# A decoder layer on one core: earlier loads, transposes over two banks, and a projection done bank by bank

## The chip, the cores and the metric

The kernel runs on one core of a Trainium2 chip. The metric is the device time of one execution in microseconds, taken as the median of several runs. The engines have short names: PE (TensorE, matmuls and transposes; PEld is its weight load), ACT (ScalarE), DVE (VectorE), POOL (GpSimd), SP (SyncE, which issues the DMAs here).

## What is computed

One layer of a hybrid decoder over x of 2048 tokens by 1024 features, in float32. Both mixers share one input projection; their outputs share one output projection.

```python
u = rmsnorm(h, attn_pre_norm[i])
proj = u @ w_in[i]
hq, hf, hi, hg, sq, sk, sv = jnp.split(proj, splits, axis=-1)
o_hg = hgrn2_mix(hq, hf, hi, lb_all[i])                # gated linear recurrence, 4 heads of 128
o_hg = rmsnorm(o_hg, hg_out_norm[i]) * jax.nn.silu(hg)
o_sb = stick_breaking_mix(sq, sk, sv)                  # strictly causal attention, 8 heads of 64
o_sb = rmsnorm(o_sb, sb_out_norm[i])
mix = jnp.concatenate([o_hg, o_sb], axis=-1) @ w_out[i]
h = h + rmsnorm(mix, attn_post_norm[i])
u = rmsnorm(h, ffn_pre_norm[i])
gate, up = jnp.split(u @ w_gate_up[i], [D_FF], axis=-1)
y = (jax.nn.silu(gate) * up) @ w_down[i]
h = h + rmsnorm(y, ffn_post_norm[i])
h = h + (p[i] @ ple_proj[i]) * jax.nn.sigmoid(h @ ple_gate[i])
```

## The kernel before

The 2048 tokens are worked on in four groups (`GT` = 512 tokens, four tiles of 128). A matmul keeps float32 accuracy by splitting each operand into a high and a low part (`split`, `weight`: ACT casts the high part, DVE or POOL subtracts to get the low one, in turn) and adding three products (`mm3`, L221 to L223). So each weight tile of 128x512 costs one DMA, one cast and one subtraction; there are four raw buffers and three pairs for it.

The order on PE is the order of the code; the other engines' instructions are put in order by the framework's planner, which goes by an estimate of their times and by the buffers that are free. The code is written as generators ("streams"). `weave` runs one main stream and lets others step in between: a slot has two half slots, a main step follows each, and a stream with phase 0 or 1 steps only at every first or second half slot, while one with phase None is spread over all. `Rate` deals out the total number of steps of a stream over several weaves.

The stages that the change touches, in order of time, with names used below:

- start: `in_norm(0)` loads x of group 0, squares it with a sum (ACT), takes the root (POOL) and scales (ACT); `in_u` transposes it (L294, PE) into PSUM banks and splits it. Before all this `build_masks` makes small masks in a pool of its own that is closed again.
- a0, a1, a2, a3: input projection of a group for keys, queries, values. b0 to b3: the same for the recurrence's inputs. Beside them run the attention (`attention`: scores into "z", a scan on DVE, a product on POOL at L413, transposes into the bank "tr", evicted by ACT at L424 and DVE at L426, values into "av") and, from a2 on, the recurrence of a group (`hgrn`, 45 steps a group, all in the bank "hg"; a step's matmuls read products that POOL at L540 and DVE at L542 update after the step before).
- the joints: in the last three slots of b0 and b1, `in_u` for the group after the next, two chunks of four transposes per slot, all into "tr", the last two after the weave.
- o0 to o3: the output projection of a group (`out_proj`, operands loaded by `out_load`). It has 8 parts of 48 matmuls of 256 columns; a part takes two banks, loads two weight tiles one after the other, goes over both banks with each, and at its end evicts both (ACT at L643 or DVE at L645). After the first part the rows' sums of squares are formed in the bank "tr" (four one-column matmuls, two DVE copies, two POOL operations). Beside o0, o1 and the first half of o2 run the rest of attention and recurrence; beside o1, o2 and o3 the normalisation of the group before (`post_mix`), and in the second halves of o1 and o2 the turning of its result (`turn`, L688, also in "tr").
- then gate and up, down, and the gated embedding, which don't change.

There are eight PSUM banks: three "mm", two "z", one each of "av", "tr", "hg". SBUF tiles rotate by tag: "ev" has 12 buffers of 128x512 (evictions, mix, gb), "xt" has 8 (x, turned tiles, temporary results of gate_up).

Of the kernel before, what the change touches and what calls it, by code (L numbers as in the profile page):

```python
# [15 lines left out]
P = 128  # L16
# [44 lines left out]
def build_masks(nc, pool, masks):  # L61

    I32 = mybir.dt.int32

    def itile(name):
        return pool.tile([P, BL], I32, tag=name, name=name)
# [18 lines left out]
def hybrid_block(  # L85
# [77 lines left out]
    with tc.tile_pool(name="mtmp", bufs=1) as mtmp:  # L163
        build_masks(nc, mtmp, masks)
# [107 lines left out]
    def in_norm(g):  # L272
        toks = []
        for t in range(TT):
            halves = [xt(), xt()]
            r0 = g * GT + t * P
            for j in range(2):
                if g == 0:
                    with tc.high_priority():
                        nc.sync.dma_start(halves[j], x[r0:r0 + P, j * GT:(j + 1) * GT])  # L280
                else:
                    nc.sync.dma_start(halves[j], x[r0:r0 + P, j * GT:(j + 1) * GT])
            r = row_rstd(halves)
# [327 lines left out]
    def out_proj(g, res):  # L611
        ops, acc = res["o"], res["oss"]
        r_hg, r_sb = [], []
        mix = [[None, None] for _ in range(TT)]
        for quarter in range(4):
# [4 lines left out]
            for part in range(2):  # L620
# [7 lines left out]
                if quarter == 0 and part == 0:  # L628
                    b = bank("tr")
                    for t in range(TT):  # L630
                        nc.tensor.matmul(b[:, t:t + 1], acc[:, t * P:(t + 1) * P], ones1, start=True, stop=True)
                    rr = const.tile([P, 2 * TT], F32, tag="rg", name="rg", bufs=2)
                    nc.vector.tensor_copy(rr[:, 0:TT], hgss[:, g, :])
                    nc.vector.tensor_copy(rr[:, TT:], b[:, 0:TT])
                    nc.gpsimd.tensor_scalar(rr, rr, 1.0 / (HH * P), EPS, op0=ALU.mult, op1=ALU.add)
                    nc.gpsimd.tensor_tensor(rr, rr, neghalf.to_broadcast((P, 2 * TT)), op=ALU.pow)
                    r_hg = [rr[:, t:t + 1] for t in range(TT)]
                    r_sb = [rr[:, TT + t:TT + t + 1] for t in range(TT)]
                for t in range(TT):
                    b = banks[t // 2][:, t % 2 * 256:(t % 2 + 1) * 256]  # L640
                    d = mix[t][half][:, o * 256:(o + 1) * 256]
                    if part == 0:
                        nc.scalar.activation(d, b, AF.Copy, scale=r_hg[t])  # L643
                    else:
                        nc.vector.scalar_tensor_tensor(d, b, r_sb[t], d, op0=ALU.mult, op1=ALU.add)  # L645
                yield
        res["mix"] = mix

    def post_mix(g, mix):
        gb = [ev(name="gb") for _ in range(2)]  # L650
# [453 lines left out]
    class Rate:  # L1104
# [14 lines left out]
    u1 = Stream(in_u(in_norm(1), us[1], ["z", "av", "tr", "hg"]))  # L1119
    main = Stream(in_proj(0, us[0], KQV))  # L1120
# [9 lines left out]
    rest = units[3] - LAG  # L1130
# [3 lines left out]
        ("a", 3, 36, 21), ("b", 2, 48, 26), ("b", 3, 48, 38),  # L1134
# [3 lines left out]
    for n, (kind, g, att_n, hg_n) in enumerate(plan):  # L1138
# [4 lines left out]
        ra, rh = Rate(att_stream, 2, att_n, slots), Rate(hg, 1, hg_n, slots)  # L1143
# [5 lines left out]
        tail = 3 if nxt else 0  # L1149
# [7 lines left out]
        if n in (3, 5):  # L1157
            hg.drain()
    todo = total_units - spent + LAG + 1
    turned = []  # L1160
# [4 lines left out]
    tt0, tt1, ss0, ss1 = {}, {}, {}, {}  # L1165
    for g in range(NG - 1):
# [3 lines left out]
        if g == 0:  # L1170
            weave(op, 6, rates.part(6), r2.part(6, 1))
            hgs[2].drain()
            weave(op, OP_SLOTS - 6, rates.part(OP_SLOTS - 6), r3.part(OP_SLOTS - 6, 1))
        elif g == 1:
            weave(op, half, rates.part(half), r3.part(half, 1), (pm, TT, 0))
            tu = Stream(turn(un_s[0], u_s[0], g_ffn, "tr", xt, ev))
            weave(op, half, rates.part(half), r3.part(half, 1), (tu, 9, 0))
        else:
            weave(op, half, rates.part(half), r3.part(half, 1), (pm, TT, 0))
# [4 lines left out]
            mm_tags[:] = ["mm", "z", "mm", "z", "mm", "av"]  # L1184
            out_load(NG - 1, res[NG - 1])
# [87 lines left out]
```

## Time and profile before

| | us |
|---|---|
| median of 3 runs | 3137.79 |
| lowest, highest | 3131.59, 3140.38 |
| the profiled execution | 3140.98 |
| its span, first to last instruction | 3139.2 |

Everything in the next sections comes from the one profiled execution. Times in the trace count from the first instruction. A matmul's row covers its way through the array, so neighbouring matmuls overlap in the trace; what counts is when PE stands idle, and at which clock it runs (PEclk 1.00 is 2.4 GHz, 0.50 is 1.2 GHz; a stage's figure is a mean of the two).

### The profile page before, as it was taken

How to read it: one execution, taken by the hardware profiler on the slowest of the kernel's cores; microseconds unless marked ns; L12 is line 12 of the kernel's file. 1: busy time of each engine (PE TensorE's matmuls, PEld its weight loads, DVE VectorE, ACT ScalarE, POOL GpSimd, SP SyncE). 2: the span in 40 equal slices, each digit the busy share in tenths (PEclk: the TensorE clock that was granted, in tenths of full speed). 3: DMA queues.
4: the chain of work that ended last, by engine and by line, in shares of the span. 5: the costliest groups of instructions: out<-in, count | busy, mean ns of one | idle time of the engine just before them, and what ended most of it. 6: DMA issues, size and time to landing. Idle time of an engine off the chain costs nothing. (4 is left out here: it accounts for less than half of the span.)

```text
span 3139.2 us, 52948 instructions
## 1 busy us (share of the span) xinstructions
PE 2927.5 (93%) x18280; PEld 2455.3 (78%) x18280; DVE 2030.1 (65%) x2793; ACT 1587.0 (51%) x3187; POOL 1622.3 (52%) x1606
## 2 busy tenths in 40 slices
PE   7999899989999989778889999999999999998979
PEld 6888688868887878767767887888788888887757
DVE  3556566657677666654686677756786676746474
ACT  5666556656666666656543332355433333545432
POOL 3344355535556555755664444455744343657364
PEclk9999899989999999899999999999999999999989
DMA  6775465446445444546766676777855664678774
GB/s 189 224 212 163 128 182 162 146 134 174 150 142 156 145 138 118 182 134 228 239 219 208 228 246 220 225 230 221 290 185 186 204 217 132 220 221 278 253 258 148
DMA packets 463822, 607.02 MB, mean 193 GB/s; under 512 B 43456, under 2 KB 269760, under 8 KB 463552
## 3 DMA queue, kind: packets, MB, share of 16 engines
q1 hardware_dynamic: 463552, 603.63, 61.1%
q8 instruction: 144, 2.36, 0.3%
q14 instruction: 126, 1.03, 0.1%
HBM read 444.61 MB, written 158.86 MB: 192 GB/s over the span
## 5 line engine op out<-in xcount | busy, mean ns | idle before, releaser
L754 ACT CAST wh<-wr 128x512 fp32r<-128x512 f32 x600 | 354.1, 618 | 544.1 <-PE mm L222 165.6
L413 POOL TENSOR_TENSOR a<-be,ring 128x512 f32<-128x512 f32 (+2 forms) x320 | 314.0, 981 | 497.8 <-DVE ring L409 473.5
L755 POOL TENSOR_TENSOR wl<-wr,wh 128x512 fp32r<-128x512 f32 x256 | 370.4, 1454 | 360.9 <-ACT wh L754 343.6
L221 PE MATMUL mm<-uh,wh 128*128 128x512 f32 x1168 | 485.5, 416 | 4.4 <-DVE c L762 2.7
L223 PE MATMUL mm<-uh,wl 128*128 128x512 f32 x1168 | 461.8, 395 | 1.6 <-POOL wl L755 1.6
L222 PE MATMUL mm<-ul,wh 128*128 128x512 f32 x1168 | 461.2, 395 | 0.0
L755 DVE TENSOR_TENSOR wl<-wr,wh 128x512 fp32r<-128x512 f32 x344 | 313.0, 915 | 178.9 <-ACT wh L754 163.0
L221 PE MATMUL mm<-wh,uh 128*128 128x256 f32 (+1 forms) x1024 | 323.3, 316 | 9.0 <-ACT mix L643 6.4
L409 DVE TENSOR_TENSOR_SCAN ring<-z,ring,be 128x512 f32<-128x512 f32 x192 | 245.9, 1281 | 100.6 <-ACT z L395 96.9
L222 PE MATMUL mm<-wl,uh 128*128 128x256 f32 (+1 forms) x1024 | 306.7, 299 | 1.7 <-POOL wl L755 1.7
L223 PE MATMUL mm<-wh,ul 128*128 128x256 f32 (+1 forms) x1024 | 305.8, 299 | 0.0
L426 DVE TENSOR_TENSOR al<-tr,ah 128x512 fp32r<-128x512 f32 (+1 forms) x320 | 192.4, 601 | 113.3 <-ACT ah L424 112.6
L223 PEld LDWEIGHTS mm<-uh,wl 128*128 128x128 f32 x1168 | 222.2, 190 | 51.7 <-POOL wl L755 2.0
L221 PEld LDWEIGHTS mm<-uh,wh 128*128 128x128 f32 x1168 | 223.4, 191 | 46.9 <-DVE c L762 3.6
L207 ACT CAST wh<-wr 128x512 fp32r<-128x512 f32 x288 | 177.9, 618 | 151.9 <-PE mm L222 79.2
L222 PEld LDWEIGHTS mm<-ul,wh 128*128 128x128 f32 x1168 | 223.2, 191 | 38.6
L208 POOL TENSOR_TENSOR wl<-wr,wh 128x512 fp32r<-128x512 f32 x144 | 187.5, 1302 | 84.1 <-ACT wh L207 78.9
L394 ACT ACTIVATE be<-z 128x512 f32<-128x512 f32 (+2 forms) x320 | 170.9, 534 | 103.2 <-PE z L388 50.3
L221 PEld LDWEIGHTS mm<-wh,uh 128*128 128x128 f32 x1024 | 201.9, 197 | 17.8 <-ACT mix L643 7.2
L424 ACT CAST ah<-tr 128x512 fp32r<-128x512 f32 (+1 forms) x320 | 167.3, 523 | 95.6 <-PE tr L421 91.4
L222 PEld LDWEIGHTS mm<-wl,uh 128*128 128x128 f32 x1024 | 202.4, 198 | 7.3 <-POOL wl L755 2.0
L223 PEld LDWEIGHTS mm<-wh,ul 128*128 128x128 f32 x1024 | 201.9, 197 | 3.9
(287 smaller groups left out, 7256.5 us busy)
## 6 DMA issues: line engine op xcount, KB each, us to landing
wr<-in_w_gate_up_dram SPq DMA_DIRECT2D x308, 256.0 KB, 3.9
wr<-in_w_in_dram SPq DMA_DIRECT2D x224, 256.0 KB, 3.3
wr<-hid_s SPq DMA_DIRECT2D x154, 256.0 KB, 3.0
wr<-in_w_down_dram SPq DMA_DIRECT2D x110, 256.0 KB, 3.4
wr<-h_s SPq DMA_DIRECT2D x96, 256.0 KB, 4.3
hid_s<-hs SPq DMA_DIRECT2D x88, 256.0 KB, 3.1
wr<-wd_s SPq DMA_DIRECT2D x88, 256.0 KB, 3.5
kt<-k_s SPq DMA_DIRECT2D x80, 256.0 KB, 3.0
```

Source lines behind the costliest of these rows:

```text
L207: nc.scalar.copy(hi, src)
L208: (lo_engine or nc.gpsimd).tensor_tensor(lo, src, hi.bitcast(F32), op=ALU.subtract)
L221: nc.tensor.matmul(o, l[0], r[0], start=start, stop=False)
L222: nc.tensor.matmul(o, l[0], r[1], start=False, stop=False)
L223: nc.tensor.matmul(o, l[1], r[0], start=False, stop=stop)
L394: nc.scalar.activation(be[:, :n], z[:, :n], AF.Sigmoid, scale=0.125)
L409: nc.vector.tensor_tensor_scan(r[:, o:o + n][:, ::-1], z[:, :n][:, ::-1], be[:, :n][:, ::-1], init, op0=ALU.mult, op1=ALU.bypass)
L413: nc.gpsimd.tensor_tensor(a[:, :n], be[:, :n], r[:, o + 1:o + n + 1], op=ALU.mult)
L424: nc.scalar.copy(hi[:, lo_c:], tr[:, lo_c:])
L426: nc.vector.tensor_tensor(lo[:, lo_c:], tr[:, lo_c:], hi[:, lo_c:].bitcast(F32), op=ALU.subtract)
L754: nc.scalar.copy(hi, src)
L755: lo_engine.tensor_tensor(lo, src, hi.bitcast(F32), op=ALU.subtract)
```

## The change

- The masks are built after the x loads of groups 0 and 1, in a buffer of attention's tag "be"; their own pool is gone. For group 0 the scaling goes from ACT to DVE.
- At the joints the chunks go to "hg" and "tr" in turn; the recurrence has its steps before the joint.
- The plan gives attention 4 more units in a3, 4 in b2 and 6 in b3, and the recurrence 42 steps (38) in b3. The rest of both is spread over o0 and o1 alone (2.5 projections before). In b3, o0 and o1 the recurrence steps at half slots (phase None) instead of every second one.
- `dense_op` takes the place of `dense` in the output projection: both weight tiles are prepared first, then one bank is filled and evicted, then the other. The sums of squares come first.
- gb of `post_mix` lies in "xt" instead of "ev".
- o2 runs without attention and recurrence. The loads of group 3's operands stand at its start, and the first splits for gate_up step in its second half.

```diff
+    room = pool.tile([P, GT], I32, tag="be", name="room")
+    used = [0]
+
     def itile(name):
-        return pool.tile([P, BL], I32, tag=name, name=name)
+        used[0] += BL
+        return room[:, used[0] - BL:used[0]]
...
-    with tc.tile_pool(name="mtmp", bufs=1) as mtmp:
-        build_masks(nc, mtmp, masks)
...
+    def dense_op(w_cols, act):
+
+        ws = [weight(w_cols(kk)) for kk in range(0, HH, 2)]
+        banks = []
+        for i in range(2):
+            banks.append(mm_bank())
+            for kk in range(HH):
+                mv = [t[:, kk % 2 * 256:(kk % 2 + 1) * 256] for t in ws[kk // 2]]
+                for j in range(2):
+                    mm3(banks[i][:, j * 256:(j + 1) * 256], cut(act[kk], 2 * i + j), mv,
+                        kk == 0 and j == 0, kk == HH - 1 and j == 1)
+                if kk == 1:
+                    yield None
+            yield banks[i]
...
             for h in halves:
-                nc.scalar.activation(h, h, AF.Copy, scale=r)
+                if g == 0:
+                    nc.vector.tensor_scalar(h, h, r, None, op0=ALU.mult)
+                else:
+                    nc.scalar.activation(h, h, AF.Copy, scale=r)
...
+        sums(acc)
         mix = [[None, None] for _ in range(TT)]
...
-                for banks in dense(HH, src, ops[part * HH:(part + 1) * HH], False):
-                    if banks is None:
+                bank_no = 0
+                for b in dense_op(src, ops[part * HH:(part + 1) * HH]):
+                    if b is None:
                         yield
...
-        gb = [ev(name="gb") for _ in range(2)]
+        gb = [xt("gb") for _ in range(2)]
...
+    build_masks(nc, att, masks)
...
-        ("a", 3, 36, 21), ("b", 2, 48, 26), ("b", 3, 48, 38),
+        ("a", 3, 40, 21), ("b", 2, 52, 26), ("b", 3, 54, 42),
...
-        weave(main, slots - tail, ra.part(slots - tail), rh.part(slots - tail, 1))
+        weave(main, slots - tail, ra.part(slots - tail), rh.part(slots - tail, 1 if hg_n < slots else None))
+        if n in (3, 5):
+            hg.drain()
         if nxt:
-            un = Stream(in_u(toks, us[nxt], ["tr"]))
-            weave(main, tail, ra.part(tail), (un, 2 * tail, 0), rh.part(tail, 1))
+            un = Stream(in_u(toks, us[nxt], ["hg", "tr"]))
+            weave(main, tail, ra.part(tail), (un, 2 * tail, 0))
...
-    rates = Rate(att_stream, 2, todo, 2 * OP_SLOTS + OP_SLOTS // 2)
-    r2 = Rate(hgs[2], 1, HG_STEPS - 38, 6)
-    r3 = Rate(hgs[3], 1, HG_STEPS, 2 * OP_SLOTS + OP_SLOTS // 2 - 6)
+    rates = Rate(att_stream, 2, todo, 2 * OP_SLOTS)
+    r2 = Rate(hgs[2], 1, HG_STEPS - 42, 2)
+    r3 = Rate(hgs[3], 1, HG_STEPS, 2 * OP_SLOTS - 2)
...
-            weave(op, half, rates.part(half), r3.part(half, 1), (pm, TT, 0))
             hgs[3].drain()
             att_stream.drain()
             side.close()
             big[0] = ctx.enter_context(tc.tile_pool(name="bigr", bufs=1, side="right"))
             mm_tags[:] = ["mm", "z", "mm", "z", "mm", "av"]
+        else:
             out_load(NG - 1, res[NG - 1])
-            for prod in (1, 2):
-                for k in range(ND // 2):
-                    t_first(0, tt0, prod, k)
+            weave(op, half, (pm, TT, 0))
             tu = Stream(turn(un_s[1], u_s[1], g_ffn, "tr", xt, ev))
-            weave(op, half - 1, (tu, 9, 0))
+            weave(op, half, (tu, 9, 0), (Stream(first_operands()), ND, 1))
```

## Rows read from the trace of the kernel before

**Rows 1.** The page's first part: PE busy, share of the span.

```profile
PE 2927.5 (93%) x18280; PEld 2455.3 (78%) x18280; DVE 2030.1 (65%) x2793; ACT 1587.0 (51%) x3187; POOL 1622.3 (52%) x1606
```

**Rows 2.** Busy time by stage (start, a0, b0, b1, b3, o0-o3): from:to, length, engines, PEclk, DMA.

```profile
0.00:29.25 29.25, 7.38 (x33) 6.50 (x33) 12.48 (x28) 17.65 (x37) 10.45 (x39) 1.00 0.56 157
29.25:101.20 71.95, 70.85 (x422) 62.70 (x420) 22.63 (x35) 40.46 (x83) 21.51 (x30) 1.00 0.76 219
...
202.20:366.35 164.15, 149.04 (x831) 124.87 (x830) 92.53 (x124) 99.19 (x205) 67.10 (x73) 0.96 0.52 157
...
478.18:671.28 193.10, 180.50 (x1404) 149.43 (x1402) 123.83 (x174) 117.91 (x250) 95.69 (x125) 0.96 0.48 147
...
972.12:1168.07 195.95, 182.30 (x1754) 150.97 (x1752) 133.78 (x192) 124.21 (x259) 116.20 (x141) 0.98 0.47 139
1168.07:1268.57 100.50, 89.38 (x939) 80.89 (x938) 61.25 (x99) 62.14 (x137) 59.65 (x74) 0.96 0.44 131
1268.57:1398.09 129.52, 101.86 (x1041) 91.35 (x1039) 75.56 (x111) 80.41 (x179) 81.67 (x108) 0.91 0.48 155
1398.09:1492.97 94.88, 77.25 (x706) 72.31 (x704) 49.96 (x72) 58.73 (x126) 59.63 (x66) 0.89 0.64 217
1492.97:1556.48 63.51, 50.04 (x395) 49.14 (x394) 41.21 (x54) 34.48 (x79) 38.02 (x43) 0.92 0.75 251
```

**Rows 3.** Timeline of the start: start, length, engine, line, operation, idle before.

```profile
0.72 0.43 SPq L145 DMA_DIRECT2D g_pre<-in_attn_pre_norm_dram  x1
...
9.22 0.19 DVE L81 TENSOR_TENSOR mask<-ge,lt 128x32 uint8<-128x32 int32 x1
9.49 3.66 SPq L280 DMA_DIRECT2D xt<-in_x_dram  x8
9.84 0.69 DVE L208 TENSOR_TENSOR wl<-wr,wh 128x512 fp32r<-128x512 f32 x1 [0.42 <-ACT wh L207]
...
16.04 1.32 ACT L285 ACTIVATE xt<-xt,rstd 128x512 f32<-128x512 f32 x2
```

**Rows 4.** PE's waits in 202 to 671: who for whom, total us, times, longest.

```profile
PE tr L294 <- DVE ul L297: 14.9, 8, 2.8
PE tr L294 <- DVE al L426: 8.3, 5, 2.4
```

**Rows 5.** PE's waits in 972 to 1557 (b3 to o3).

```profile
PE hg L503 <- POOL qp L540: 13.6, 5, 5.7
PE tr L688 <- DVE al L426: 10.3, 6, 2.3
PE tr L688 <- ACT ev L694: 7.1, 3, 3.5
...
PE mm L221 <- ACT mix L643: 6.4, 2, 5.4
...
PE av L222 <- DVE wl L208: 3.6, 1, 3.6
...
PE z L222 <- DVE wl L208: 3.3, 1, 3.3
...
PE hg L503 <- DVE small L506: 1.9, 2, 1.0
```

**Rows 6.** Timeline of two recurrence steps in b3 and their last products.

```profile
1107.40 0.46 PE L503 MATMUL hg<-qp,ks 128*32 128x32 f32 x32
...
1108.41 0.81 POOL L540 TENSOR_TENSOR qp<-qp,tree 128x256 f32<-128x256 f32 x1
...
1127.93 1.05 PE L553 MATMUL hg<-v,q 128*128 128x128 f32 x8
...
1131.25 0.35 DVE L563 SCALAR_TENSOR_TENSOR sl<-st,tree,hg 128x128 f32<-128x128 f32 x1
```

**Rows 7.** Groups by line in o3 (1493 to 1557): count, busy us, mean ns, idle before.

```profile
L208 POOL TENSOR_TENSOR wl<-wr,wh 128x512 fp32r<-128x512 f32 x7 | 9.8, 1407 | 7.1 <-ACT wh L207 7.0
...
L208 DVE TENSOR_TENSOR wl<-wr,wh 128x512 fp32r<-128x512 f32 x7 | 8.0, 1147 | 0.5 <-ACT wh L207 0.5
```

More of the change, by code (lines that the diff above doesn't have):

```diff
@@ L613, in out_proj, with sums @@
         r_hg, r_sb = [], []
+        def sums(acc):
+            b = bank("tr")
+            for t in range(TT):
+                nc.tensor.matmul(b[:, t:t + 1], acc[:, t * P:(t + 1) * P], ones1, start=True, stop=True)
+            rr = const.tile([P, 2 * TT], F32, tag="rg", name="rg", bufs=2)
+            nc.vector.tensor_copy(rr[:, 0:TT], hgss[:, g, :])
+            nc.vector.tensor_copy(rr[:, TT:], b[:, 0:TT])
+            nc.gpsimd.tensor_scalar(rr, rr, 1.0 / (HH * P), EPS, op0=ALU.mult, op1=ALU.add)
+            nc.gpsimd.tensor_tensor(rr, rr, neghalf.to_broadcast((P, 2 * TT)), op=ALU.pow)
+            r_hg.extend(rr[:, t:t + 1] for t in range(TT))
+            r_sb.extend(rr[:, TT + t:TT + t + 1] for t in range(TT))
+        sums(acc)
         mix = [[None, None] for _ in range(TT)]
@@ L623, in src @@
                     return w_out[r:r + 2 * P, c:c + 256]
-                for banks in dense(HH, src, ops[part * HH:(part + 1) * HH], False):
-                    if banks is None:
+                bank_no = 0
+                for b in dense_op(src, ops[part * HH:(part + 1) * HH]):
+                    if b is None:
                         yield
[L628 to L646, printed above, removed]
+                        continue
+                    for n in range(2):
+                        t = 2 * bank_no + n
+                        d = mix[t][half][:, o * 256:(o + 1) * 256]
+                        bn = b[:, n * 256:(n + 1) * 256]
+                        if part == 0:
+                            nc.scalar.activation(d, bn, AF.Copy, scale=r_hg[t])
+                        else:
+                            nc.vector.scalar_tensor_tensor(d, bn, r_sb[t], d, op0=ALU.mult, op1=ALU.add)
+                    bank_no += 1
+                    yield
         res["mix"] = mix
     def post_mix(g, mix):
-        gb = [ev(name="gb") for _ in range(2)]
+        gb = [xt("gb") for _ in range(2)]
         for j in range(2):
@@ L1128, in hybrid_block @@
     hg_now = idle
-    rest = units[3] - LAG
     plan = [
@@ L1142, in hybrid_block @@
         hg = hgs[hg] if hg is not None else idle
-        ra, rh = Rate(att_stream, 2, att_n, slots), Rate(hg, 1, hg_n, slots)
+        tail = 3 if kind == "b" and g + 2 < NG else 0
+        ra, rh = Rate(att_stream, 2, att_n, slots), Rate(hg, 1, hg_n, slots - tail)
         spent += att_n
@@ L1148, in hybrid_block @@
             out_load(0, res[0])
-        tail = 3 if nxt else 0
-        weave(main, slots - tail, ra.part(slots - tail), rh.part(slots - tail, 1))
+        weave(main, slots - tail, ra.part(slots - tail), rh.part(slots - tail, 1 if hg_n < slots else None))
+        if n in (3, 5):
+            hg.drain()
         if nxt:
-            un = Stream(in_u(toks, us[nxt], ["tr"]))
-            weave(main, tail, ra.part(tail), (un, 2 * tail, 0), rh.part(tail, 1))
+            un = Stream(in_u(toks, us[nxt], ["hg", "tr"]))
+            weave(main, tail, ra.part(tail), (un, 2 * tail, 0))
             main.drain()
@@ L1156, in hybrid_block, with first_operands @@
         main.drain()
-        if n in (3, 5):
-            hg.drain()
     todo = total_units - spent + LAG + 1
-    turned = []
-    rates = Rate(att_stream, 2, todo, 2 * OP_SLOTS + OP_SLOTS // 2)
-    r2 = Rate(hgs[2], 1, HG_STEPS - 38, 6)
-    r3 = Rate(hgs[3], 1, HG_STEPS, 2 * OP_SLOTS + OP_SLOTS // 2 - 6)
+    rates = Rate(att_stream, 2, todo, 2 * OP_SLOTS)
+    r2 = Rate(hgs[2], 1, HG_STEPS - 42, 2)
+    r3 = Rate(hgs[3], 1, HG_STEPS, 2 * OP_SLOTS - 2)
     half = OP_SLOTS // 2
     tt0, tt1, ss0, ss1 = {}, {}, {}, {}
+    def first_operands():
+        for prod in (1, 2):
+            for k in range(ND // 2):
+                t_first(0, tt0, prod, k)
+                yield
     for g in range(NG - 1):
@@ L1170, in hybrid_block @@
         if g == 0:
-            weave(op, 6, rates.part(6), r2.part(6, 1))
+            weave(op, 2, rates.part(2), r2.part(2))
             hgs[2].drain()
-            weave(op, OP_SLOTS - 6, rates.part(OP_SLOTS - 6), r3.part(OP_SLOTS - 6, 1))
+            weave(op, OP_SLOTS - 2, rates.part(OP_SLOTS - 2), r3.part(OP_SLOTS - 2))
         elif g == 1:
-            weave(op, half, rates.part(half), r3.part(half, 1), (pm, TT, 0))
+            weave(op, half, rates.part(half), r3.part(half), (pm, TT, 0))
             tu = Stream(turn(un_s[0], u_s[0], g_ffn, "tr", xt, ev))
-            weave(op, half, rates.part(half), r3.part(half, 1), (tu, 9, 0))
-        else:
-            weave(op, half, rates.part(half), r3.part(half, 1), (pm, TT, 0))
+            weave(op, half, rates.part(half), r3.part(half), (tu, 9, 0))
             hgs[3].drain()
@@ L1184, in hybrid_block @@
             mm_tags[:] = ["mm", "z", "mm", "z", "mm", "av"]
+        else:
             out_load(NG - 1, res[NG - 1])
-            for prod in (1, 2):
-                for k in range(ND // 2):
-                    t_first(0, tt0, prod, k)
+            weave(op, half, (pm, TT, 0))
             tu = Stream(turn(un_s[1], u_s[1], g_ffn, "tr", xt, ev))
-            weave(op, half - 1, (tu, 9, 0))
+            weave(op, half, (tu, 9, 0), (Stream(first_operands()), ND, 1))
             for k in range(ND // 2):
```

## The prediction

> **What bounds the kernel now.** I read the page first: PE is busy 93% of the span, far ahead of the other engines [rows 1]. So time can be won only where PE stands idle or runs at the lower of its two clocks (1.2 instead of 2.4 GHz), and the next question is where. Busy time by stage answers it [rows 2]; idle is length minus PE busy. The start (to the first projection matmul) has 29.25 - 7.38 = 21.9 us. The two stages b0 and b1, whose ends transpose the next group's x (the joints), have 15.1 and 12.6, with a mean clock of 0.96. b3 has 13.7, and the four output projections o0 to o3 have 11.1, 27.7, 17.6 and 13.5, with clocks of 0.96, 0.91, 0.89, 0.92. These eight stages hold 133 us; the change touches each of them. What is lost to the clock I take as length x (1 - clock): b0 6.6, b1 7.7, b3 3.9, o0 to o3 4.0 + 11.7 + 10.4 + 5.1 = 31.2. It overlaps the idle time in part, so it is an upper bound. Then I asked, stretch by stretch, which wait ends last: at the start [rows 3], at the joints [rows 4], in b3 to o3 [rows 5, 6]; and what weights cost in o3 [rows 7]. The 1582 us after o3 (gate and up, down, gated embedding) keep their code.
>
> **Start.** SyncE issues the first x load at 9.49, right behind the last mask operation at 9.22, though its queue had begun at 0.72 [rows 3]: x lies where the mask builder's scratch lay. Without that pool the loads carry the highest priority and nothing holds them. Bounds: 8.8 earlier, if they go ahead of the six column loads at 0.72, and 0, if something else in the queue still holds them. I take 8 because of the priority mark, and since the columns that could go first are few. The eight scalings leave ScalarE (1.32 for two [rows 3], 5.3 in all), which also does eight squares; after the change the squares run at the pace of the landings, and only the last scaling stays on the path. I take 2 of the 5.3; bounds 0 and 5.3. A DVE scaling of this shape has no row; nearest is a DVE subtraction of 128x512 at 0.69 [rows 3], about ScalarE's 0.66. The mask work moves behind group 1's x loads: two POOL iotas and 20 DVE operations, about 8 us on DVE, in a stage where PE is busy 70.85 of 71.95 [rows 2] and DVE 22.63; cost nothing. If the cover failed, those 8 us would delay DVE evictions there. First users: attention, which gets its scratch buffer back, 70 us later. The weight loads now stand behind 2 MB of x; they are needed only after the transposes. **-10 us** (-2 to -14).
>
> **Joints.** Two chunks of transposes (L294) follow each other in a slot into the single "tr" bank, which attention also uses: the first waits for attention's eviction (L426: 8.3 us in 5 waits), the second for the first's (L297: 14.9 in 8) [rows 4]. Such pairs come four times per joint; these waits are 23 of the 27.7 us that b0 and b1 idle. With "hg" and "tr" in turn the first chunk goes at once and the second finds "tr" free about when the first does today: the second wait goes, the first stays. The recurrence must leave "hg" first: its last 24 steps run in 29 slots instead of 32, still at most one per slot, and cost nothing. I take 16 of 23 us (bounds 8 and 20), and 7 of the 14.3 us of clock (bounds 2 and 12). **-23**.
>
> **Recurrence at half slots.** A step's matmuls need the products that the step before released on POOL and DVE. Today steps fall on one half slot in two; where a rate exceeds one per slot, two stand back to back. Counting the rates: 6 such pairs in b3 (38 steps in 32 slots), 1 + 11 in the projections (7 in 6, 45 in 34). The trace has exactly 18 waits in the seven rows of "hg", 38.4 us together, of which the first and the last stand in [rows 5]. Afterwards no two share a half slot, but 52 of the 90 steps follow in the next one (20 in b3, 32 in o0 and o1), some 2.8 us of PE work later (b3: 182.3 / 64; o0: 89.4 / 32 [rows 2]). An ordinary step is ready 1.8 us after its start (1107.40 to 1109.22), so it fits; the state chain takes 3.7 (1127.93 to 1131.60) and does not [rows 6]. Estimate: 5 of the 52 are state chains, late by 0.9, and a fifth of the others is late by 1.5, since POOL and DVE are busy 60% here: 19 us. **-19** (bounds -34 and +16).
>
> **Output projection by banks.** Today a part fills two of three banks and evicts both at its end, so the next part soon meets a bank not yet released: 6.4 us in two waits, 5.4 of it in o3 [rows 5]. The 5.4 also holds a shortage of "ev" buffers, which moving gb to "xt" eases. Both go: **-6**. The price is in the weights. Of three pairs of buffers two now serve the whole part: a part's second weight reuses a pair freed 24 matmuls before its need, where today it is 48. At 50.04 us for 384 in o3 [rows 2] that is 3.1 us for a ScalarE cast and a subtraction; every second weight goes to POOL, 1.41 there [rows 7]. On ScalarE the cast waits in order, and the squares and evictions behind it wait too. In o0 and o1 attention and recurrence double the 3.1. In o2 and o3, 16 parts, I take 0.5 us each: **+8** (0 to +40). Means of 1.15 on DVE and 1.41 on POOL in o3 [rows 7], against 0.69 for a DVE subtraction at the start [rows 3], say that the two subtractions hinder each other. The Trainium skill (SBUF — State Buffer, "Who interferes with whom") has the rule that speaks against this change: a VectorE instruction with two SBUF inputs and a GpSimd instruction reading SBUF exclude each other, and the later one waits out the whole of the other. The means in [rows 7] agree. By the rule a POOL subtraction that waits out one of DVE ends 0.69 + 1.41 = 2.1 us after the cast, still under 3.1, and the sum stays; with more in front of it, it is rival A.
>
> **The row sums first.** Four one-column matmuls, two DVE copies and two POOL operations move to each projection's head. Their input was loaded one projection earlier. Attention's wait for their bank stays, at another place: 0.
>
> **Attention over two projections.** Fourteen units (4 in a3, 4 in b2, 6 in b3) and a few recurrence steps leave the projections for stages where PE is the bound: the same PE work elsewhere, 0. o2 loses attention and recurrence. Left on PE there: 46 us of matmuls (at most the 50.04 of o3) and 3 of transposes. ScalarE had 58.7 busy there and POOL 59.6 [rows 2]; without attention and recurrence but with all of the loads of group 3 (moved to o2's start, eight loads ahead of post_mix's in SyncE's queue) I estimate 47 to 50 each. Three engines of equal load don't mesh fully: **+8** (0 to +15). The 7.1 us in which o2's turning transposes waited for ScalarE [rows 5] came from two turns in one slot; now there are eight slots for nine: **-7** (-7 to 0). In o1 the 10.3 us behind attention's eviction [rows 5] stay.
>
> **gb in "xt"** (8 buffers): gb and four tokens want ten, so later tokens' loads wait for earlier ones. No matmul of o1 to o3 waits for them; where post_mix of group 3 meets gate_up, which uses "xt" too, 0, bounds -8 and +8.
>
> **Clock in b3 to o3:** 35 us today with 84 us idle. The idle falls by about a third: **-10** (-20 to 0).
>
> **Sum:** -10 - 23 - 19 - 6 + 8 + 8 - 7 - 10 = -59. The profiled execution took 3140.98 (span 3139.2), so 3082; it lay 3.2 above the median, so 3079 for the median.
>
> **Rivals.** A: slower. The 3.1 us don't suffice and nearly every part stalls on its second weight as o3 did twice, 3.6 and 3.3 us [rows 5], though it had double the slack. o3 lost 5.1 us of clock on 13.5 idle, 0.38 per us. 24 parts (o2, o3 and half of o0 and o1) x 3.5 x 1.38 = 116, instead of +8: 3079 + 108 = 3187. It turns slower from about 2.0 us of wait per part (24 x 2.0 x 1.38 = 66 eats 59 + 8). For it: the means in [rows 7]. Against: in o0 and o1 other matmuls stand in between, and o3 had two such waits in eight parts, not eight. B: the half slot is too short. Half of the 52 close steps wait 2.1 us like a pair today: 55 instead of 19, 3115. For it: DVE and POOL 60% busy; against: the 1.8 us. C: the moves do less than they say; x still goes behind columns and weights (-5), and the joints stay bound by attention's eviction (-8 in all): 3079 + 5 + 15 = 3099. D: gains and new waits cancel, about 3138.
>
> **How the numbers follow.** Forecast 0.74, A 0.06, B 0.09, C 0.06, D 0.05. A measurement of this kernel tells some 0.3% (9.4 us) from nothing. Faster: forecast, B and C, 0.89; same: D, 0.05; slower: A, 0.06. The term bounds give 3030 to 3140 if all fall on one side; the forecast's own spread is about 3045 to 3110, and with B and C inside 3045 to 3115 leaves out A, D and the tails.
>
> **What would show it.** Right: first x load before 5 us, first projection matmul near 19; at the joints one wait per pair, on attention's eviction; few waits above 2 us on "hg"; no wait on mix; o2 near 62 us, o0 to o3 together near 345 instead of 388. Wrong: many waits of o2 and o3 on wl or wh (A); dozens of short waits on "hg" (B); x loads after weights (C).

## The result, and the profile after

The changed kernel takes 3111.1 us (median of four runs, 3108.9 to 3112.1), the kernel before beside it 3134.7 (3129.9 to 3140.4): a ratio of 0.9923, interval 0.9903 to 0.9943. So it is faster, by 24 us, and the range held the time; but the forecast was 3079, a gain of 59. The profiled execution took 3112.1 (span 3110.3), where 3082 was forecast for it. The 30 us between the two are what has to be found.

The first part of the page, which answers to [rows 1]: busy time, share of the span, instructions. PE's share rose by one point.

```profile
PE 2918.1 (94%) x18280; PEld 2440.2 (78%) x18280; DVE 2034.7 (65%) x2801; ACT 1584.4 (51%) x3180; POOL 1632.3 (52%) x1606
```

Busy time by stage, as [rows 2], for the start, a0 to b3, o0 to o3, and all that follows: from:to, length, then busy time and instructions of PE, PEld, DVE, ACT and POOL, PEclk, DMA share, GB/s.

```profile
0.00:20.82 20.82, 7.50 (x32) 6.62 (x33) 8.91 (x34) 12.93 (x28) 10.93 (x39) 1.00 0.65 169
...
194.88:349.80 154.92, 146.25 (x832) 123.17 (x829) 89.31 (x122) 97.33 (x202) 67.14 (x73) 0.98 0.55 165
349.80:459.12 109.32, 108.35 (x1033) 92.03 (x1032) 72.24 (x111) 68.98 (x147) 56.55 (x72) 1.00 0.62 178
459.12:640.97 181.85, 175.50 (x1403) 146.00 (x1401) 125.10 (x174) 117.57 (x250) 95.39 (x125) 0.99 0.52 156
640.97:777.92 136.95, 134.60 (x1176) 111.20 (x1175) 98.94 (x144) 90.25 (x196) 73.34 (x96) 1.00 0.56 157
777.92:962.61 184.69, 178.41 (x1431) 146.84 (x1430) 130.15 (x174) 124.03 (x260) 107.97 (x128) 1.00 0.49 146
962.61:1163.44 200.83, 194.46 (x1849) 157.17 (x1840) 145.13 (x208) 135.74 (x286) 126.68 (x150) 0.99 0.49 143
1163.44:1265.49 102.05, 92.70 (x1048) 83.46 (x1047) 70.90 (x110) 64.18 (x140) 71.37 (x87) 0.97 0.42 129
1265.49:1379.13 113.64, 93.49 (x1038) 83.87 (x1038) 61.52 (x100) 68.43 (x150) 72.44 (x89) 0.94 0.49 163
1379.13:1461.78 82.65, 55.40 (x426) 53.97 (x426) 26.83 (x38) 46.26 (x97) 45.85 (x53) 0.83 0.69 231
1461.78:1522.96 61.18, 51.77 (x387) 49.75 (x386) 42.92 (x54) 33.56 (x77) 40.25 (x45) 0.94 0.80 265
1522.96:3110.34 1587.38, 1510.31 (x6634) 1238.77 (x6632) 1079.56 (x1406) 619.02 (x1120) 801.62 (x575) 0.97 0.68 219
```

The start is 8.4 us shorter, b0 9.2, b1 11.2 and a2 between them 2.5. a3 to b3 are 25.7 us longer: that is the attention moved there, with four recurrence steps (PE is busy 26.0 us longer in the three). o0 to o3 take 359.5 us instead of 388.4; 345 were forecast, and one row misses by more than those 14.5 us: o2 takes 82.65 us instead of the 62 of the forecast, PE stands still in 27 of them, and its clock is 0.83. The other parts of the 30 us: a3 and b2 idle 8.6 instead of 1.7, the stages behind o3, whose code is the same, are 4.7 longer, and the start is 1.6 short of its mark.

The waits of PE in b0 to b1 (as [rows 4]) and in b3 to o3 (as [rows 5]): who waits for whom, total us, times, longest.

```profile
PE tr L314 <- DVE al L446: 6.6, 5, 2.0
PE tr L441 <- DVE ul L317: 6.3, 5, 2.0
...
PE tr L715 <- DMA xt<-un_s: 15.6, 2, 12.6
PE av L458 <- DVE al L446: 8.2, 7, 3.2
PE z L224 <- POOL wl L210: 7.9, 6, 3.4
PE av L224 <- POOL wl L210: 7.5, 1, 7.5
...
PE hg L523 <- POOL qp L560: 6.3, 3, 4.0
PE tr L715 <- DVE al L446: 3.2, 2, 1.6
```

The second chunk's wait at the joints (14.9 us in [rows 4]) is gone and the first chunk's stayed, at 6.6; attention now waits 6.3 for "tr" in its turn (0.9 before). All waits on "hg" come to 13.6 us in 11 (18 waits and 38.4 us in [rows 5]), and no wait on mix is left. What is new is the first of these rows in b3 to o3: the transposes of `turn` wait 15.6 us for a DMA from `un_s`, the normalised rows that `post_mix` writes to DRAM.

**What o2 waits for.** PE's three long waits in o2, and rows of the other engines ahead of them: start, length, operation, idle before and its releaser.

```profile
1396.64 5.38 POOL L782 TENSOR_TENSOR ul<-wr,uh 128x512 fp32r<-128x512 f32 x4
1398.81 0.19 ACT L275 ACTIVATION_READ_ACCUMULATOR junk<-h 128x1 f32 x1
...
1401.98 1.71 POOL L210 TENSOR_TENSOR wl<-wr,wh 128x512 fp32r<-128x512 f32 x1
1403.75 0.58 PE L224 MATMUL av<-wl,uh 128*128 128x256 f32 x1 [7.54 <-POOL wl L210]
...
1408.64 0.33 POOL L277 TENSOR_TENSOR ssum<-ss 128x1 f32<-128x1 f32 x2
...
1413.10 1.34 ACT L692 ACTIVATE mix<-h,rstd 128x512 f32<-128x512 f32 x2 [2.26 <-POOL rstd L269]
1419.56 0.41 PE L715 MATMUL tr<-ident,xt 128*128 128x128 f32 x2 [2.94 <-DMA xt<-un_s]
1420.19 1.33 ACT L692 ACTIVATE mix<-h,rstd 128x512 f32<-128x512 f32 x2 [0.51 <-POOL rstd L269]
1426.99 1.33 ACT L692 ACTIVATE mix<-h,rstd 128x512 f32<-128x512 f32 x2 [0.47 <-POOL rstd L269]
1427.74 0.93 SPq L693 DMA_DIRECT2D un_s<-mix  x2
1429.85 3.44 SPq L703 DMA_DIRECT2D xt<-un_s  x7
1432.59 0.69 PE L715 MATMUL tr<-ident,xt 128*128 128x128 f32 x2 [12.62 <-DMA xt<-un_s]
```

Read from below. The transposes at 1432.59 need the load of 1429.85, that needs the store of 1427.74, and that the scaling of the group's last token tile at 1426.99. The last three of the four tiles come through this chain about 7 us apart (1413.10, 1420.19, 1426.99): square, row sum and root on ACT and POOL, gain on DVE, addition on POOL, square and root again, scaling on ACT. The first was scaled at 1388.71, and the second came late: ACT had its sums at 1399.00, and POOL adds them only at 1408.64, behind a run that is mostly subtractions for the first operands of gate and up (L782; two other operations of 128x512 stand among them). The same run delays a weight's low part and so the matmul at 1403.75. Before the change PE had attention and recurrence to do over this chain, and no matmul of o2 waited for `un_s`; now the chain lies bare.

### The profile page after: what moved, and what is told of

Read it like the earlier page. It is cut to its first block, busy times and chain, and to the rows that moved or that the text cites. A ratio compares the mean times of both kernels' runs of the same rounds, so it can differ in the third digit from the quotient of the medians.

```text
span 3110.3 us, 52961 instructions
## 1 busy us (share of the span) xinstructions
PE 2918.1 (94%) x18280; PEld 2440.2 (78%) x18280; DVE 2034.7 (65%) x2801; ACT 1584.4 (51%) x3180; POOL 1632.3 (52%) x1606
## 5 line engine op out<-in xcount | busy, mean ns | idle before, releaser
L782 POOL TENSOR_TENSOR wl<-wr,wh 128x512 fp32r<-128x512 f32 x256 | 370.5, 1454 | 369.6 <-ACT wh L781 360.4
L782 DVE TENSOR_TENSOR wl<-wr,wh 128x512 fp32r<-128x512 f32 x344 | 314.1, 919 | 167.3 <-ACT wh L781 145.6
L223 PE MATMUL mm<-wh,uh 128*128 128x256 f32 (+1 forms) x992 | 309.7, 312 | 2.3 <-ACT wh L781 2.2
L224 PE MATMUL mm<-wl,uh 128*128 128x256 f32 (+1 forms) x992 | 294.0, 296 | 2.9 <-POOL wl L782 2.6
L225 PE MATMUL mm<-wh,ul 128*128 128x256 f32 (+1 forms) x992 | 292.9, 295 | 0.0
L223 PEld LDWEIGHTS mm<-uh,wh 128*128 128x128 f32 x1168 | 221.7, 190 | 44.6 <-issue 2.6
L223 PEld LDWEIGHTS mm<-wh,uh 128*128 128x128 f32 x992 | 191.7, 193 | 10.7 <-ACT wh L781 3.1
L224 PEld LDWEIGHTS mm<-wl,uh 128*128 128x128 f32 x992 | 192.2, 194 | 8.7 <-POOL wl L782 3.6
L225 PEld LDWEIGHTS mm<-wh,ul 128*128 128x128 f32 x992 | 191.7, 193 | 3.8
```

What stands on the lines that cost most here:

```text
L223: nc.tensor.matmul(o, l[0], r[0], start=start, stop=False)
L224: nc.tensor.matmul(o, l[0], r[1], start=False, stop=False)
L225: nc.tensor.matmul(o, l[1], r[0], start=False, stop=stop)
L782: lo_engine.tensor_tensor(lo, src, hi.bitcast(F32), op=ALU.subtract)
```

## The experiments

All times are medians, their ratios are to the kernel before, and each kernel is the changed one with the edit shown.

**The first operands' subtractions off POOL** (e_first_vec):

```diff
-            tt[prod, k] = pair_of(t_blk(grp, prod - 1, 0, k), "u", prod, G)
+            tt[prod, k] = pair_of(t_blk(grp, prod - 1, 0, k), "u", prod, V)
```

> The changed kernel, with the subtractions of gate_up's first operands (products 1 and 2, eight of 128x512) in o2 on DVE instead of POOL. Theory POOL order: those eight stand ahead of a weight's subtraction and of post_mix's roots on POOL; they make both the 7.5 us wait and the 12.6 us wait of o2 (82.7 us long). Both together fall below 4, o2 comes to 62 to 66, the whole to 3111 - 18 = 3093. Theory dependency: the turn of group 1 is asked for before post_mix's chain through DRAM (some 7 us for each of four tokens) can be done, whatever POOL does. The 7.5 goes, 8 or more of the 12.6 stay, o2 about 73, the whole 3101.

**The turn after the first operands** (e_turn_late):

```diff
-            weave(op, half, (tu, 9, 0), (Stream(first_operands()), ND, 1))
+            weave(op, half // 2, (Stream(first_operands()), ND, 1))
+            weave(op, half // 2, (tu, 9, None))
```

> The changed kernel, with the turn of group 1 in the last four slots of o2 instead of the last eight; POOL keeps its work. Theory dependency: the waits of the turning transposes (2.9 and 12.6) fall below 4 together, the 7.5 on the weight stays, o2 about 69, the whole 3111 - 13 = 3098. Theory POOL order alone: post_mix is so late that half of the 12.6 is only met later, o2 76, the whole 3105.

Measured: 3105.4 (ratio 0.989 to 0.992) and 3104.5 (0.9887 to 0.9919), some 6 us better than the changed kernel each, with intervals that overlap its own. In e_first_vec, the stage o2, and what the turn waits for in it:

```profile
1378.91:1454.59 75.68, 53.32 (x426) 51.96 (x426) 33.88 (x46) 45.85 (x97) 38.00 (x45) 0.86 0.77 253
```

```profile
PE tr L715 <- DMA xt<-un_s: 19.3, 2, 17.0
```

```profile
1426.12 0.69 PE L715 MATMUL tr<-ident,xt 128*128 128x128 f32 x2 [16.97 <-DMA xt<-un_s]
```

In e_turn_late, the stages o2 and o3, and the same wait:

```profile
1376.65:1447.74 71.09, 56.14 (x426) 54.08 (x426) 26.48 (x37) 46.38 (x96) 48.57 (x55) 0.90 0.75 256
1447.74:1512.25 64.51, 51.32 (x387) 48.93 (x386) 41.15 (x56) 33.79 (x78) 38.12 (x43) 0.95 0.78 266
```

```profile
PE tr L715 <- DMA xt<-un_s: 1.4, 1, 1.4
```

With POOL free, the 7.5 us wait for the weight's low part is gone (1.0 is left) and o2 is 7 us shorter, but the turn waits 3.7 us more than before: PE came earlier to the same chain. The chain itself ends sooner: its second tile is scaled at 1399.60 instead of 1413.10, its last at 1420.10 instead of 1426.99, and the turn goes on at 1426.12 instead of 1432.59; those 6.5 us are o2's gain. So neither theory holds alone, and 3105.4 is above what either gave: POOL's order made the chain some 7 us longer, and the rest of its length stays. With the turn later, the wait for the chain falls from 15.6 to 1.4 and o2 by 11.6 us, of which o3 gives back 3.3; the wait for the weight's low part stays (7.6), as the first theory said. That is the chain shown as the cause of the turn's wait. The kernel gains only 6.6 of it; the profiled execution, the longest of its four runs (3109.0), is 7.6 us longer behind o3, and I can't say why, the code there is the same.

**Attention again over two and a half projections** (u_att), **and the plan's numbers alone** (p_plan: the first edit without the rest):

```diff
-        ("a", 3, 40, 21), ("b", 2, 52, 26), ("b", 3, 54, 42),
+        ("a", 3, 36, 21), ("b", 2, 48, 26), ("b", 3, 48, 42),
...
-    rates = Rate(att_stream, 2, todo, 2 * OP_SLOTS)
+    rates = Rate(att_stream, 2, todo, 2 * OP_SLOTS + OP_SLOTS // 2)
...
+        else:
+            weave(op, half, rates.part(half), (pm, TT, 0))
             att_stream.drain()
...
-        else:
             out_load(NG - 1, res[NG - 1])
-            weave(op, half, (pm, TT, 0))
```

> The changed kernel with attention's plan of before (36, 48, 48 units) and its rest over two and a half projections; the recurrence stays as changed. Theory: the two-projection plan only moves PE work (26 us into a3, b2, b3) and pays for it with new waits there (7 us) and in o2 (20 us), so undoing it shortens a3, b2, b3 by 25 to 33, lengthens o0 to o2 by about as much less some 10 to 15 us of waits: the whole 3097 to 3103. Rival (the prediction's own sum, in which this part cost nothing net): 3111 within 4.

> The attention part split: only its plan numbers go back (36, 48 and 48 pieces in a3, b2 and b3 instead of 40, 52 and 54), the attention still ends with the second output projection. With the whole part undone the stages lost 18.8 us, all of it waits: 10.3 in a3 to b3, 14.4 in o2, and o0 and o1 gained 4.6 of waits. Theory 'two costs': a3 to b3 lose their 10 us of waits, o0 and o1 (fourteen more pieces) take back 3 to 6, o2 keeps its 27 us of waits and its length of 80 to 84: 3104 to 3108. Rival 'the plan alone': o2 shortens too, 3093. Rival 'the waits only move': o0 and o1 take back all 10 us, 3109 to 3113.

Measured: 3092.7 (0.9846 to 0.9879) and 3104.4 (0.9885 to 0.9923). This part of the change costs 18 us, more than either theory had: without it the kernel is faster, by intervals that don't touch. The stages a3, b2 and o2 of u_att:

```profile
642.71:769.94 127.23, 127.18 (x1141) 106.74 (x1140) 92.70 (x135) 84.63 (x184) 69.40 (x91) 1.00 0.56 161
769.94:943.18 173.24, 171.59 (x1409) 142.90 (x1407) 121.81 (x165) 115.78 (x243) 99.98 (x121) 1.00 0.50 155
...
1360.55:1443.43 82.88, 70.05 (x484) 66.65 (x484) 34.38 (x48) 50.26 (x104) 45.24 (x50) 0.86 0.64 215
```

Set the last row against o2 of the changed kernel: 82.88 us with 70.05 of PE work, and 82.65 with 55.40. The 14.65 us of attention that were taken out of o2 bought nothing there; PE waits in their place, and they are paid a second time where they went. In a3 and b2 that is more than their own work, too: PE idles 8.6 us there in the changed kernel and 1.7 here. The row for it, in a3 and b2 of the changed kernel:

```profile
PE av L458 <- DVE al L446: 7.4, 16, 0.9
```

Sixteen short waits for DVE's low parts of attention's weights: with 13 pieces in eight slots or a little more, instead of 12, DVE comes late with some of them. What it does ahead of them I did not look up. In p_plan a3 and b2 idle 1.8 us, as in u_att, but its o2 has the fault of the changed kernel:

```profile
1370.43:1450.84 80.41, 57.28 (x426) 56.11 (x426) 25.36 (x40) 45.51 (x97) 45.08 (x52) 0.85 0.72 237
```

So "the plan alone" is out. Against "the waits only move": PE idles 6.8 us less in a3 to b3 than in the changed kernel and only 1.5 more in o0 and o1. By medians 6.7 of the 18.4 us are the plan's and 11.7 those of an o2 without attention, each some 3 us uncertain. The 11.7 is clear of noise (the intervals of p_plan and u_att don't touch), the 6.7 is not by itself: the intervals of p_plan and the changed kernel overlap. The 11.7 shows in o0 and o1, which carry o2's attention in p_plan and are 11.1 us longer there than in u_att, while its o2 is only 2.5 shorter.

**The gain rows again in "ev"** (u_gb), where mix and the evictions lie, **and the same without the attention part** (c_att_gb):

```diff
-        gb = [xt("gb") for _ in range(2)]
+        gb = [ev(name="gb") for _ in range(2)]
```

> The changed kernel with gb of post_mix in ev again. Theory: gb in xt holds two of eight buffers that gate_up's first temporaries need too, so the last tokens of group 3's post_mix load late; the waits at the start of gate_up (4.6 and 16.8 us) fall to the 13 us in all that stood there in the kernel before, and o3 gets its 5 us wait on mix back: the whole 3111 - 8 + 5 = 3108. Rival: those waits come from the order of t_second's work on ACT and DVE; then they stay near 21 us and the whole is 3116.

> The attention part undone and the gain rows of post_mix again in their own buffers (ev). Theory 'xt is short at the start of gate_up': the 16.9 us wait of the first gate_up product falls to some 6, the rest is near 1580 instead of 1588, and the kernel takes 3085 to 3089. Rival 'the gain rows cost nothing': 3091 to 3095, the gate_up wait is 16 to 17 again.

Measured: 3104.4 (0.9891 to 0.9924) and 3081.0 (0.9815 to 0.9844). Against u_att the second gains 11.7 us, and the intervals don't touch. PE's waits in the 77 us behind o3, of the changed kernel and of c_att_gb:

```profile
PE av L223 <- ACT wh L781: 21.4, 2, 16.8
```

```profile
PE av L225 <- DVE wl L782: 6.5, 2, 5.7
PE av L223 <- ACT wh L781: 6.4, 1, 6.4
```

The wait of 16.8 us for one weight of gate and up is 6.4 without the two "xt" buffers for gb (all waits there: 14.8 instead of 21.4), and the stages behind o3 take 1581.0 us instead of 1588.4 in u_att; where the other 4 of the 11.7 us come from these rows don't tell. `post_mix` of group 3 and gate and up draw on the same eight buffers, and the loads stand in one queue. Which of the loads is held up I did not single out, so that buffers are short there is the likely reason, not one that is shown. The theory of the second run holds for the wait and for the stages behind o3; both times came out lower than expected. In "ev" gb has a price too, which the change had taken away: in o2 and o3 of u_gb PE waits for mix again.

```profile
PE mm L223 <- ACT mix L669: 11.1, 2, 8.2
```

With attention in o2 (c_att_gb) this wait is 2.0. In the changed kernel the two prices of gb stand against each other: "ev" is 6.7 us better by medians, with intervals that overlap.

**The two edits of o2 once more, in c_att_gb** (c_att_gb_vec, c_att_gb_late):

> As the one before, and the subtractions of gate_up's first operands go from POOL to DVE. In the kernel without the attention change o2 has 14 us of waits of the output projection for POOL's low parts of the weights. Theory 'order on POOL': these fall to 4 or less and o2 is 8 to 10 us shorter, 3077 to 3081. Rival 'DVE, which still has the attention's low parts in the first half of o2, is late instead': less than 3 us, 3083 to 3089.

> As the second, and in the second half of o2 the first operands come first and the turn after them. In the kernel as changed this brought o2 from 82.7 to 71.1 us, since the turn stood waiting for the chain of post_mix through DRAM. Without the attention change no matmul of the turn waits for that chain any more (no such row in o2). Theory 'the attention covers the chain': nothing is left to gain, 3084 to 3091, and the last turn is pushed into o3. Rival 'the order helps for itself': 3077 to 3081.

Measured: 3080.8 (0.9801 to 0.9847) and 3079.4 (0.9804 to 0.9837), which the intervals don't tell from the 3081.0 of c_att_gb. With attention over the chain its wait in c_att_gb is 4.7 us and no more:

```profile
PE tr L715 <- DMA xt<-un_s: 4.7, 1, 4.7
```

So neither POOL's order nor the place of the turn is worth anything that the medians show. Both times lie in the ranges of the theories that gave the order a price of its own (3077 to 3081), but only because c_att_gb, without either edit, lies there as well. The theory of an order on POOL had counted on 14 us of waits for low parts; in o2 of c_att_gb there are 3.7, and 0.3 with the edit. In the profiled executions o2 is some 6 us shorter with either edit (77.2 and 76.1 for 82.8); as the four runs of the first spread from 3072.8 to 3085.8, a gain of that size is neither shown nor ruled out.

**The parts undone one at a time.** u_joint:

```diff
-            un = Stream(in_u(toks, us[nxt], ["hg", "tr"]))
+            un = Stream(in_u(toks, us[nxt], ["tr"]))
```

> The changed kernel with the joint's chunks all in the bank tr again (the recurrence still ends before). If the second bank gives what b0, b1 and a2 got shorter (22.9 us in all in the profile), the whole is 3111 + 20 = 3131, with waits on L314 in b0 and b1 near 23 us. If a part of that gain came from elsewhere (the recurrence leaving the joint, other orders), 3118 to 3124.

u_start, the scalings back on ACT and the masks back in a pool ahead of the loads:

```diff
+    with tc.tile_pool(name="mtmp", bufs=1) as mtmp:
+        build_masks(nc, mtmp, masks)
...
-                if g == 0:
-                    nc.vector.tensor_scalar(h, h, r, None, op0=ALU.mult)
-                else:
-                    nc.scalar.activation(h, h, AF.Copy, scale=r)
+                nc.scalar.activation(h, h, AF.Copy, scale=r)
...
-    build_masks(nc, att, masks)
```

> The changed kernel with the mask builder and its pool before the loads again and the scaling of group 0 on ACT. First projection matmul back near 29.2 instead of 20.8: the whole 3111 + 8.4 = 3119.5, nothing else moved by more than 2 us.

Measured: 3134.5 (0.9985 to 1.0009) and 3119.6 (0.9929 to 0.9962). The joints are worth 23.4 us and the start 8.5, near the forecast (23 and 10). u_joint brings back the row of [rows 4], 14.4 us in 8 waits for the second chunk, and b0 and b1 are as long as before (163.90 and 192.72 us), so the second bank alone had shortened them:

```profile
PE tr L314 <- DVE ul L317: 14.4, 8, 2.3
```

**The recurrence again at one half slot in two**, in the changed kernel (u_hg) and in c_att_gb (c_hg):

```diff
-        weave(main, slots - tail, ra.part(slots - tail), rh.part(slots - tail, 1 if hg_n < slots else None))
+        weave(main, slots - tail, ra.part(slots - tail), rh.part(slots - tail, 1))
...
-            weave(op, 2, rates.part(2), r2.part(2))
+            weave(op, 2, rates.part(2), r2.part(2, 1))
```

and so for the three weaves of r3.

> The changed kernel with the recurrence on every second half slot again (same counts of steps per stage, so 10 pairs back to back in b3, 1 in the first two slots of o0 and 15 after). Theory: a pair waits about 2.1 us as before, 26 pairs, so the waits on hg go from 13.5 to some 55 us and the whole to 3111 + 35 to 45 = 3146 to 3156. Rival: elementwise engines follow the new order and the waits stay below 30 us: 3125.

> The kernel without the attention change and with its own buffers for the gain rows (3081), and in it the recurrence again on one half slot in two. In the kernel as changed this cost 35 us, where the prediction had 19. Theory 'the denser plan makes the half slots worth more': with the plan of before it costs 15 to 25, 3096 to 3106. Rival 'the half slots are worth 35 for themselves': 3112 to 3120.

Measured: 3146.3 (1.0021 to 1.0043) and 3127.6 (0.9965 to 0.999): 35 and 47 us. The time of the first run is the one that its theory gave (3146), with fewer waits on "hg" than it counted on (41.4 us for 55). Both theories of the second run miss; a less dense attention does not make the half slots cheaper to give up. The count explains why both are above 19. The change also packs the recurrence closer, and these two kernels keep that: 42 steps in the 32 slots of b3, 3 in 2 and 45 in 30 of the projections make 10 + 1 + 15 = 26 pairs that share a half slot, where the kernel before had 18. The traces have 26 waits on "hg" in u_hg (41.4 us in b3 to o1) and 27 in c_hg (44.6 us), against 11 (13.6 us) in the changed kernel and 9 (9.1 us) in c_att_gb. So undoing the half slots prices them above what they gained over the kernel before; for that the waits of the two kernels stand side by side, 38.4 against 13.6. That c_hg loses 11 us more than u_hg lies in part in another wait, of the row sums and the turn for the bank "tr" behind attention's evictions. In b3 to o1 of c_hg it is 26.0 us, where c_att_gb has 7.2; in u_hg it is 15.7, where the changed kernel has 3.9:

```profile
PE tr L638 <- DVE al L446: 14.4, 2, 7.4
PE tr L715 <- DVE al L446: 11.6, 6, 2.9
```

The clock of o0 and o1 is lower as well, 0.90 and 0.89 where c_att_gb has 0.95 in both. Why these waits grow more there is not settled.

**The projection again by pairs of banks**, the row sums still first, in the changed kernel (u_dense) and in c_att_gb (c_dense):

```diff
-                for b in dense_op(src, ops[part * HH:(part + 1) * HH]):
+                for banks in dense(HH, src, ops[part * HH:(part + 1) * HH], False):
```

with the evictions of all four tiles at the part's end.

> The changed kernel with the output projection in pairs of banks again (sums of squares still first, gb still in xt, six banks in o2 and o3). By the prediction's terms the order by banks saved the two waits on mix and cost stalls on weights: undone, the waits on wl and wh in o2 and o3 (about 20 us) halve, no wait on mix returns in o2 and o3 since six banks turn there, at most 3 us in o0 and o1: the whole 3103 to 3108. Rival: bank by bank is worth more than its stalls, since two evictions at once delay the next part: 3114 to 3120.

> The same kernel (3081), and in it the output projection again by pairs of banks, with the row sums still first. In the kernel as changed this cost 7 us, and its o2 waited 32 us for the turn's operands. Theory 'the price was the uncovered chain of o2': with attention in o2 it costs nothing, within 4 us of 3081. Rival 'evicting bank by bank is worth 7 for itself': 3086 to 3092. Rival 'the weights were dearer, as predicted': 3073 to 3078.

Measured: 3118.5 (0.9927 to 0.9962) and 3080.3 (0.9803 to 0.9843). So projecting bank by bank is worth 7 us in the changed kernel, by medians whose intervals overlap, and nothing where attention covers o2, as the theory of the second run said. There it trades one wait for another: in o0 to o3 of c_dense PE waits 18.8 us for mix and 0.9 for low parts of weights, in c_att_gb 2.0 and 12.4. In the first run the time is the rival's, but not for the rival's reason: waits on mix come to 4.0 us in u_dense, while the turn waits for the chain twice as long (26.8 of these 31.8 us in o2, where the changed kernel has 15.6):

```profile
PE tr L711 <- DMA xt<-un_s: 31.8, 3, 13.7
```

Undone one at a time, the parts sum to 8.5 + 23.4 + 35.2 + 7.4 - 18.4 - 6.7 = 49 us, where the change gained 24. With the 25 us of waits in place of the 35.2 for the half slots and 0 for the banks it is 32; the 8 that are left are about what six differences of medians, each uncertain by some 3 us, leave open.

## Why the prediction was right and wrong, step by step

- **Start, -10:** right in the main part, the loads; 8.4 us in the stage, 8.5 undone. The first load of x is issued at 0.72 (9.49 in [rows 3]), 8.8 earlier; the first projection matmul is at 20.8, for 19. So the 2 us for the scalings did not show: the first of them, at 9.67, waits for its root, which POOL takes only behind the second tile's sum (8.25). The mask work did not go to a0; it lies in the start itself, from 5.7 us on, and no matmul waits for it.
- **Joints, -23:** right in mechanism, the first wait of a pair staying and the second going. That the size is exact is luck in part: of the 23.0 us by which b0, a2 and b1 are shorter, 13.2 are idle time (for 16 of waits), as attention's new wait for "tr" was not foreseen, and 9.8 are PE's work at a higher clock (for 7).
- **Half slots, -19:** right in mechanism, too small. 24.8 us of waits on "hg" went, 13.6 are left for an estimated 19, and three of the 11 that are left are over 2 us. Rival B, dozens of short waits, has no row.
- **Bank by bank, -6 and +8:** the waits on mix went as said. Waits for weights in o2 and o3 rose from 8.0 us (3.6 and 3.3 in [rows 5], and 1.1) to 21.0, 13 for a forecast of 8; 7.5 of them are the one wait behind POOL's run of first operands, which I had not looked for on POOL's queue. Rival A, a stall in nearly every part, came in number and not in size: o3 has nine waits in its eight parts, 9.4 us in all, one of them over 2 us (3.4). That is 1.2 us a part, under the 2.0 from which A would have made the kernel slower. c_dense says that the edit as a whole is worth nothing for itself.
- **Row sums first, 0:** attention's 4.9 us of waits behind the sums are gone; the sums wait 0.7 for attention's eviction in their place, and 4.5 in c_att_gb.
- **Attention over two projections, 0 + 8 - 7: this is the step that failed.** It measured +18. I balanced the busy times of PE, ACT and POOL in o2 and added 8 us for three engines that don't mesh. But what stands in o2 beside the projection is a chain, `post_mix` over DRAM into `turn`, and such a chain has a length that no engine's busy time shows: ACT was busy 46.3 of 82.7 us and POOL 45.9. The 7 us of turn waits did go as said, and 15.6 for the chain came in their place. The 0 for the units moved to stages where PE is the bound was wrong too: their work cost on PE what it cost before, but DVE's part in it came late in a3 and b2 (7.4 us of waits). ACT and POOL were about as busy in o2 as estimated (47 to 50), so the balance was right and the reckoning by it was not. In o1 the turn's 10.3 us behind attention's eviction, which were to stay, fell to 3.2.
- **gb in "xt", 0 (bounds 8 either way):** the second term that failed. I chose the middle, and the price came where I had named it and left it at nothing, at the start of gate and up: 11.7 without the attention part, beyond the bound. In the changed kernel it was 6.7, inside the bound; there gb in "ev" costs 11.1 us of waits on mix in its place.
- **Clock, -10:** the sum of length x (1 - clock) over b3 to o3 fell from 35 to 29.6, about half; o2 at 0.83 took back 3.6 of the 9.1 that the others gained.
- The rivals gave 3099 (C) and 3115 (B), on either side of the measured time; neither is what happened, since the start, the joints and the half slots did nearly their share or more. That the range held 3111 is luck: its upper end was there for B. The bounds of the terms, added up, give 3017 to 3199, and not the 3030 to 3140 of the prediction.

The version without the attention part and with gb in "ev" (c_att_gb, 3081.0) is 30 us under the changed kernel and 55 under the one before beside it (3136.1); no version was measurably faster. It stands where I had put the changed kernel, and it leaves out just the two terms that failed.

## What to carry to other kernels

Before work is moved out of a stage, follow the chains of that stage through every engine and DMA queue to the last one that PE needs, and ask what covers them now: a stage can't be shorter than its longest bare chain, whatever its engines' busy shares say (o2: 82.65 us with 55.40 of PE work). Price a part both by undoing it alone and by adding the rest without it, for a part can look good only because it mends what another broke (bank by bank, 7 us and 0). And where two stages share a buffer pool, look at their seam before a buffer more is taken from it: there a wait of 6.4 us became one of 16.8.

## What the runs showed of the hardware

Two scalings of 128x512 on DVE took 0.88 us, where ACT took 1.32 [rows 3]; I had assumed them equal.

```profile
9.67 0.88 DVE L303 TENSOR_SCALAR xt<-xt,rstd 128x512 f32<-128x512 f32 x2 [2.38 <-POOL rstd L269]
```

The Trainium skill (VectorE: DVE Perf Modes, "Mode 2×_2P — use both read ports for one tensor") says that an operation with one tensor input in SBUF can read it through both ports, in float32 as well, which an operation on two tensors can't; the row agrees, at 0.44 for one against 0.69 for a subtraction.

Of two subtractions that start together in o2, the one on DVE takes 1.78 us, and 0.68 where it is alone:

```profile
1410.85 1.26 POOL L210 TENSOR_TENSOR wl<-wr,wh 128x512 fp32r<-128x512 f32 x1
1410.87 1.78 DVE L210 TENSOR_TENSOR wl<-wr,wh 128x512 fp32r<-128x512 f32 x1 [8.30 <-ACT wh L209]
...
1572.70 0.68 DVE L782 TENSOR_TENSOR ul<-wr,uh 128x512 fp32r<-128x512 f32 x1
```

The one that starts 0.02 us later takes 1.10 us more than alone, most of the 1.26 of the other. That is the rule which the prediction weighed (the Trainium skill, SBUF — State Buffer, "Who interferes with whom"): by it the later one would end 1.26 + 0.68 = 1.94 us after the first began; the row has 1.80.

The clock in o2: from 1420.3 to 1437.3 it is granted at 0.50, that is 1.2 GHz. PE had stood still but for two transposes since 1416.6 when it fell, and PE is busy 4.71 of these 17.00 us; the rest lies in the turn's wait of 12.62 us. It rises again at 1437.3, after the matmuls have come back at 1432.59.

```profile
1420.30:1437.30 17.00, 4.71 (x22) 4.71 (x23) 1.42 (x2) 5.41 (x11) 4.62 (x8) 0.50 0.67 220
```
